# Placing two later triangular inverses behind a scan's first step, and giving each step's output matmuls a PSUM bank of their own

## The chip, the cores and the metric

The kernel runs on one core of one Trainium2 chip. The metric is the device time of one execution in microseconds (us), the median over several runs. The core has five engines with a queue each: TensorE (PE, with its weight loads shown apart as PEld), VectorE (DVE), ScalarE (ACT), GpSimd (POOL) and SyncE (SP, which issues the DMAs). An engine executes its queue in order, so an instruction that waits holds back all that stand behind it.

## What is computed

The reference is one layer of a diffusion trunk over 128 context tokens and 512 latent tokens of width 1024. Around two sub-layers stand RMS norms with shift, scale and gate. The first sub-layer sends one input projection to two mixers: an attention of 8 query heads, and RWKV-7 time mixing of 8 heads of width 64 in two directions. The second is a gated feed-forward block with a convolution of width 3 over the tokens. The part that matters here is the time mixing, which the reference writes token by token:

```python
sa = einsum('bhvk,bhk->bhv', s, -kk_t)
s = s * w_t + sa[..., None] * (kk_t * a_t) + v_t[..., None] * k_t
y = einsum('bhvk,bhk->bhv', s, r_t)
```

The layer returns both token streams, the context's keys and values, and the final states of the context's scans.

## The kernel before, in words

**Chunks instead of tokens.** The scan is taken in chunks of 64 tokens. Within a chunk the recursion is solved with the inverse of a 64 by 64 triangular matrix. Heads come in pairs, an even and an odd one on the two halves of the 128 partitions ("par"). There are three groups: `g0` (head pairs 0 and 1, 8 latent chunks), `ctx` (all four pairs, 2 context chunks) and `g1` (pairs 2 and 3, 8 latent chunks), walked in this order by each of the two directions. That makes 20 chunk steps for each direction.

**The inverses.** `inverse` (L829) makes the chunk inverses of one group. DVE transposes the group's matrix `LT` into `Lt` in four instructions (L845). `Ls` is formed from it (L854), and a row-by-row elimination follows (L870, L871), on DVE for `g0` and `ctx` and on POOL for `g1`. DVE transposes the result twice (`XT`, `XN`, L875 and L877). Eight copies put the diagonal blocks into `MT` (L889), each on DVE or ACT as the planner chose. Matmuls make `W` (L897), ACT copies it out (`Ws`, L901), matmuls make `B` (L909), and four copies bring `B` into `MT` (L912 to L915). The helper `cpy` makes such copies, so in the profile they stand on its line L377.

**Grams, decays, steps.** `s_gram` multiplies, for two chunks at once, the loaded rows `AK` (L964); it takes both banks of the PSUM ring `mi`, one for each par. DVE masks each into `GM` (L968) and ACT adds a block (L972). `s_decay` transposes the decayed rows into `DT` through one `mi` bank (L998). `s_chain` (L1033) is the dependent part of a step: it multiplies `GM` with the state and values `V_` (L1067), ACT copies that out as `Rt`, `MT` is applied (L1075), ACT scales the result to `U_` (L1080), `DT` is applied (L1089). Then the same generator issues the output: eight matmuls (L1099, L1103) into a fourth slot of the same PSUM bank `cp`. After them DVE adds the state update (L1113) into the next chunk's `V_`. The stream `out` (L1117) copies the output to `y` (first half of the steps) or adds it there (L1127), and then frees the slot (ring `yp`).

**What runs beside it.** `s_gemm2` computes the last input projections (L556, L570); their results are copied out (tile `e`, L377), stored (L464) and read back (L1265) for the attention. The attention's norms (L1289), scores (L1412), transposes (L1439) and weighted sums (L1460) follow, beside the scan, then the output projection (L1687), and from about 640 us on the feed-forward block (L1844, L2050).

**What sets the order.** Each piece of work is a generator that yields a request for an engine with an estimated duration, for a free slot of a ring, or for an event. A planner (`Flow`) resumes the generator whose request can start first, by estimated times and priorities. This gives the order of emission. A list scheduler then orders each engine's queue, by emission with boosts: `s_chain` has priority 0 and boost 200, `inverse` of `ctx` 0.1 and of `g1` 0.15 with boost 100, `s_gram` and `s_decay` 0.2, `out` 0.3 with boost 100. `behind` orders two instructions of one engine without a semaphore.

Of the kernel before, what the change touches and what calls it, by code (L numbers as in the profile page):

```python
# [47 lines left out]
def trunk(ctx: ExitStack, tc: tile.TileContext, a, o, dbg=None):  # L48
# [598 lines left out]

    G0, G1, CX = Group("g0", (0, 1), 2, 8), Group("g1", (2, 3), 2, 8), Group("ctx", (0, 1, 2, 3), 0, 2)
    groups = [G0, CX, G1]
    pt = [rc.tile([P, 4, 10], F32, name=nm("pt")) for _ in range(2)]  # L650
    bon = rc.tile([P, 10, 4], F32, name="bon")
    qm = [rf.tile([P, 10, 65], F32, name=nm("qm")) for _ in range(2)]
# [176 lines left out]
    def inverse(g, en, pl, mp, sfx, rg, bank):  # L829
        eng = ve if en == "V" else ge  # L830

        def W(n, k=1):
            return V(n, k=k) if en == "V" else G(0.99 * (k * 0.1 + 2.2e-3 * n))

        nu, LT = g.nu, g.LT
        for p in g.pairs:
            for d in range(2):
                yield ev_("ab", p, d)
        yield ring("inv" + sfx)
        Lt = pl.tile([P, 1024], F32, name=nm("Lt"), tag="i0" + sfx)  # L840
        for qd in range(4):
            pr = slice(32 * qd, 32 * qd + 32)
            t0 = 32 * (qd % 2)
            yield V(1024)
            ve.transpose(Lt[pr].rearrange("p (t s) -> p t s", s=32), LT[pr, :, t0:t0 + 32].rearrange("p u t -> p t u"))  # L845
        Ls = pl.tile([P, 32, 32], F32, name=nm("Ls"), tag="i1" + sfx)
        X = pl.tile([P, 1024], F32, name=nm("X"), tag="i2" + sfx)
        X3 = X.rearrange("p (t s) -> p t s", s=32)
        Lt3 = Lt.rearrange("p (t s) -> p t s", s=32)
        yield G(1.0)  # L850
        ge.memset(X, 0.0)
        ge.memset(X[:, ::33], 1.0)
        yield W(1024)
        eng.tensor_tensor(Ls, Lt3, Lt3.rearrange("p t s -> p s t"), ALU.add)  # L854

        yield A(496, k=12)
        Lf = Ls.rearrange("p t s -> p (t s)")
        se.copy(X[:, 32::66], Lf[:, 32::66])
        for i in range(2):
            for j in range(2):  # L860
                se.copy(X[:, 64 + 32 * i + j::132], Lf[:, 64 + 32 * i + j::132])
        for b in (4, 8, 16):
            for q in range(0, 32, 2 * b):
                se.copy(X3[:, q + b:q + 2 * b, q:q + b], Ls[:, q + b:q + 2 * b, q:q + b])
        tmp = pl.tile([P, 256], F32, name=nm("tmp"), tag="i3" + sfx)
        for s in range(1, 31):
            n = 31 - s
            yield W(2 * n * s, k=2)
            t3 = tmp[:, :n * s].rearrange("p (t j) -> p t j", j=s)
            eng.tensor_tensor(t3, Ls[:, s + 1:32, s:s + 1].to_broadcast([P, n, s]), X3[:, s:s + 1, 0:s].to_broadcast([P, n, s]), ALU.mult)  # L870
            eng.tensor_tensor(X3[:, s + 1:32, 0:s], X3[:, s + 1:32, 0:s], t3, ALU.add)  # L871
        XT = pl.tile([P, 1024], F32, name=nm("XT"), tag="i0" + sfx)
        XN = pl.tile([P, 1024], F32, name=nm("XN"), tag="i1" + sfx)
        yield V(1024)
        ve.transpose(XT, X)  # L875
        yield V(1024)
        ve.transpose(XN.rearrange("p (j u) -> p j u", u=32), X3.rearrange("p i j -> p j i"))  # L877
        XT3 = XT.rearrange("p (i u) -> p u i", u=32)
        XN3 = XN.rearrange("p (j u) -> p u j", u=32)
        MT = mp[0].tile([P, 2 * nu, 64], F32, name=nm("MT"), tag=mp[1] or "MT" + g.nm)  # L880
        g.MT = MT
        yield G(2.0)
        ge.memset(MT, 0.0)
        fw, bw = slice(0, nu), slice(nu, 2 * nu)
        qs_ = [(slice(64 * e, 64 * e + 32), slice(64 * e + 32, 64 * e + 64)) for e in range(2)]
        for e in range(2):
            q0, q1 = qs_[e]
            for dst, src in ((MT[q0, fw, 0:32], XT3[q0, fw]), (MT[q1, fw, 32:64], XT3[q1, fw]), (MT[q0, bw, 0:32], XN3[q0, bw]), (MT[q1, bw, 32:64], XN3[q1, bw])):
                e2 = yield VA(32 * nu)  # L889
                cpy(e2, dst, src)  # L890
        yield ring(rg)
        W3 = bank("W")[:, :32 * nu].rearrange("p (u j) -> p u j", j=32)
        for u in range(nu):
            if u % 4 == 0:
                yield T(0.5)
            for q0, q1 in qs_:
                te.matmul(W3[q1, u], lhsT=LT[q0, u, 32:64], rhs=XN3[q0, u], start=True, stop=True)  # L897
                te.matmul(W3[q0, u], lhsT=LT[q1, nu + u, 0:32], rhs=XT3[q1, nu + u], start=True, stop=True)
        yield A(32 * nu)
        Ws = pl.tile([P, 16, 32], F32, name=nm("Ws"), tag="i2" + sfx)  # L900
        se.copy(Ws[:, :nu], W3)  # L901
        flow.give(rg)
        yield ring(rg)
        B3 = bank("B")[:, :32 * nu].rearrange("p (u j) -> p u j", j=32)
        for u in range(nu):
            if u % 4 == 0:
                yield T(0.5)
            for q0, q1 in qs_:
                te.matmul(B3[q0, u], lhsT=Ws[q1, u], rhs=XT3[q1, u], start=True, stop=True)  # L909
                te.matmul(B3[q1, u], lhsT=Ws[q0, u], rhs=XN3[q0, nu + u], start=True, stop=True)  # L910
        for q0, q1 in qs_:
            e2 = yield VA(32 * nu)  # L912
            cpy(e2, MT[q0, fw, 32:64], B3[q0])
            e2 = yield VA(32 * nu, par=True)
            cpy(e2, MT[q1, bw, 0:32], B3[q1])  # L915
        flow.give(rg)
        flow.give("inv" + sfx)
        flow.done("inv", g.nm)
# [29 lines left out]
    def s_gram(d):  # L948

        mm = cm[:, C_MK + 128 * d:C_MK + 128 * d + 128]  # L950
        for g, i0, j, cc in two(d):
            keys = [(d, g.nm, i0, ci) for ci in cc]
            yield ev_("ak", *keys[1])
            yield ring(f"GM{d}")
            GM = rp2.tile([P, 2, 2, 2, 128], F32, name=nm("GM"), tag=f"GM{d}", bufs=2)
            yield ring("mi", 2)
            ps = [mi("gr").rearrange("p (s i t) -> p s i t", s=2, i=2) for _ in range(2)]
            yield T(1.75)
            for s, key in enumerate(keys):
                ak = akt[key]  # L960
                for i in range(2):
                    for par in range(2):
                        pr = HALF[par]
                        te.matmul(ps[par][:, s, i], lhsT=ak[pr, i, 1], rhs=ak[pr, i, 0], start=True, stop=True)  # L964
            for par in range(2):
                pr = HALF[par]
                yield V(512)
                ve.tensor_tensor(GM[:, :, par], ps[par], mm[:, None, None].to_broadcast([P, 2, 2, 128]), ALU.mult)  # L968
                flow.give("mi")
                yield A(256, k=2)  # L970
                for s, key in enumerate(keys):
                    se.copy(GM[pr, s, par, :, LO], akt[key][pr, :, 0, LO])  # L972
            for s, key in enumerate(keys):
                grams[key] = GM[:, s]
                flow.done("gm", *key)
# [53 lines left out]
            flow.done("set", g.nm)  # L1029

    cps, cpf = [], []

    def s_chain(d):  # L1033
        cp = cps[d]
# [7 lines left out]
        for g, i0, j, ci in walk(d):  # L1042
# [45 lines left out]
                    for par in range(2):  # L1088
                        order(par, te.matmul(cp[HALF[par], 2, i], lhsT=DT[:, i, HALF[par]], rhs=U_[par][:, i], start=True, stop=True))  # L1089
            flow.give(f"DT{d}")  # L1090
            yield ring(f"yp{d}")

            ak = akt.pop(key)
            yield T(0.6)

            for i in range(2):
                for par in range(2):
                    pr = HALF[par]
                    order(par, te.matmul(cp[pr, 3, i], lhsT=ak[pr, i, 0, HI], rhs=V_[par][pr, i], start=(i == 0), stop=False, skip_group_check=True))  # L1099
            for i in range(2):  # L1100
                for par in range(2):
                    pr = HALF[par]
                    order(par, te.matmul(cp[pr, 3, i], lhsT=GM[:, par, i, HI], rhs=U_[par][:, i], start=False, stop=True, skip_group_check=True))  # L1103
            flow.done("mm", *key)
            flow.add(0.3, out(g, d, i0, j, ci), 100)
            if not last and (g.nch - 1 - (j + 1)) <= j:
                yield ev_("mm", 1 - d, g.nm, i0, nxt)
            if upd:
# [5 lines left out]
            if last and g.outs[d] is not None and i0 == g.np - 2:  # L1114
                sy.dma_start(o["so"][d], g.outs[d])

    def out(g, d, i0, j, ci):  # L1117
        first = j < g.nch - 1 - j
        if not first:
            yield ev_("out", 1 - d, g.nm, i0, ci)  # L1120
        yv, yp = g.y[:, ci, i0:i0 + 2], cps[d][:, 3]
        if first:
            eng = yield OPT_E(128)
            cpy(eng, yv, yp)
        else:
            yield V(128)
            ve.tensor_tensor(yv, yv, yp, ALU.add)  # L1127
        flow.give(f"yp{d}")
        if j % 2:
            flow.give(f"GM{d}")  # L1130
            flow.give(f"AK{d}")
# [399 lines left out]
    rp2 = rp2p.__enter__()  # L1531
    flow.done("rp2")
    flow.add(PR_MOD1, s_mods1())
    for name, n in (("yp0", 1), ("yp1", 1), ("md", 1), ("GM0", 2), ("GM1", 2), ("DT0", 2), ("BD0", 1), ("BD1", 1), ("DT1", 2), ("AK0", 2), ("AK1", 2), ("gT", 2), ("set", 1), ("setx", 1)):
        flow.ring(name, n)
    rwkv = []
    for d in range(2):
# [678 lines left out]
```

## Time and profile before

| | us |
|---|---|
| median of 3 runs (lowest to highest) | 1103.17 (1098.99 to 1106.76) |
| profiled execution, its own time | 1104.36 |
| its span, first to last instruction | 1102.6 |
| mean granted TensorE clock | 0.94 of full speed |
| PE / DVE / ACT / POOL busy | 1019.5 / 790.7 / 563.4 / 507.4 |

A row of a timeline gives the start, the duration, the engine, the line, the operation, output and input, shapes and count, and in brackets the idle time before it with what ended that. A row of stages gives, for a stretch, the busy time of each engine with its number of instructions, then the granted TensorE clock, the DMA share and GB/s. A row of waits gives who waited, for whom, the us in total, how often, and the longest.

### The profile page before, as it was taken

The numbers are of one execution on the slowest core, as the hardware profiler recorded it, in microseconds if no ns is written. First come the engines' busy times: TensorE is split into PE (matmuls) and PEld (weight loads), VectorE is DVE, ScalarE is ACT, GpSimd is POOL, SyncE is SP. The second block draws the span as 40 slices with busy tenths as digits, with TensorE's granted clock in tenths as the row PEclk, the third lists the DMA queues.
The fourth block names the chain that finished last, engine by engine and source line by source line (L and its number), as shares of the span: only waits on it lengthen the run. The fifth ranks groups of instructions, "written<-read, shape, count | busy, mean of one in ns | idle before, by whom it ended". The sixth has DMA issues, their size and how long they took to land. (4 is left out here: it accounts for less than half of the span.)

```text
span 1102.6 us, 20567 instructions
## 1 busy us (share of the span) xinstructions
PE 1019.5 (92%) x8034; PEld 853.6 (77%) x8034; DVE 790.7 (72%) x1367; ACT 563.4 (51%) x1261; POOL 507.4 (46%) x446
## 2 busy tenths in 40 slices
PE   6999998778779999999999988999999998899997
PEld 3788776677665556777777888999999997788885
DVE  3536689989729777465774789999999999643324
ACT  4275433254654767476654764555555556334431
POOL 1234423567415204210202058788888888642330
PEclk8899998889857899799999999999999999899999
DMA  9414534640245684211061421222222223531202
GB/s 364 185 67 116 152 103 133 184 126 21 97 150 194 212 267 136 68 59 61 9 229 74 153 90 44 88 89 94 77 77 78 78 99 112 193 113 58 95 1 96
DMA packets 70433, 127.84 MB, mean 116 GB/s; under 512 B 15664, under 2 KB 41776, under 8 KB 67264
## 3 DMA queue, kind: packets, MB, share of 16 engines
q1 hardware_dynamic: 70336, 126.53, 34.4%
q8 instruction: 63, 1.03, 0.4%
q14 instruction: 34, 0.28, 0.1%
HBM read 105.00 MB, written 21.51 MB: 115 GB/s over the span
## 5 line engine op out<-in xcount | busy, mean ns | idle before, releaser
L1807 POOL TENSOR_TENSOR w<-raw,w 128x512 fp32r<-128x512 f32 (+1 forms) x84 | 153.9, 1839 | 142.6 <-ACT w L1806 121.4
L2050 PE MATMUL dn<-w,ah 128*128 128x512 f32 x660 | 155.7, 398 | 7.9 <-DVE c L1850 7.9
L2050 PEld LDWEIGHTS dn<-w,ah 128*128 128x128 f32 x660 | 125.1, 190 | 38.3 <-issue 8.3
L1844 PE MATMUL up<-tq,w 128*128 128x324 f32 x960 | 150.2, 312 | 2.8 <-DVE x L1989 2.8
L1844 PEld LDWEIGHTS up<-tq,w 128*128 128x128 f32 x960 | 145.2, 190 | 3.1 <-DVE x L1989 3.1
L1844 PE MATMUL up<-hq,w 128*128 128x324 f32 x864 | 137.0, 313 | 4.8 <-ACT w L1806 2.3
L1844 PEld LDWEIGHTS up<-hq,w 128*128 128x128 f32 x864 | 129.6, 188 | 7.8 <-DVE up L1992 4.6
L1807 POOL TENSOR_TENSOR w<-sw,w 128x512 fp32r<-128x512 f32 x80 | 122.4, 1551 | 8.6 <-ACT w L1806 8.6
L1924 DVE TENSOR_TENSOR ah<-act,ah 128x644 fp32r<-128x644 f32 x42 | 58.7, 1415 | 75.8 <-ACT ah L1923 75.8
L1848 ACT ACTIVATE c<-up,pv 128x322 f32<-128x322 f32 x86 | 52.1, 620 | 97.3 <-DVE up L1992 55.6
L432 POOL TENSOR_TENSOR lo<-raw,hi 128x1024 fp32r<-128x1024 f32 x17 | 42.7, 2509 | 68.4 <-ACT hi L430 66.9
L1063 POOL TENSOR_TENSOR SP<-vse,pt 64x128 f32<-64x128 f32 x36 | 14.3, 398 | 128.4 <-DVE vse L1113 127.7
L1923 ACT CAST ah<-act 128x644 fp32r<-128x644 f32 x44 | 31.8, 732 | 76.4 <-PE dn L2050 76.3
L1806 ACT CAST w<-raw 128x512 fp32r<-128x512 f32 (+1 forms) x86 | 63.2, 748 | 5.0 <-PE dn L2050 2.8
L964 PE MATMUL gr<-AK 64*128 64x128 f32 x320 | 47.4, 329 | 11.8 <-ACT DT L377 4.5
L964 PEld LDWEIGHTS gr<-AK 64*128 64x128 f32 x320 | 38.8, 222 | 21.4 <-ACT DT L377 4.7
L1687 PE MATMUL op<-wo,m 128*128 128x512 f32 x192 | 48.3, 404 | 1.7 <-DVE m L1681 1.0
L1849 DVE SCALAR_TENSOR_TENSOR c<-up,pv,c 128x322 f32<-128x322 f32 x86 | 46.5, 543 | 3.8 <-ACT c L1848 3.8
L1806 ACT CAST w<-sw 128x512 fp32r<-128x512 f32 x80 | 47.5, 620 | 2.7 <-PE up L1844 2.7
L1850 DVE SCALAR_TENSOR_TENSOR c<-up,pv,c 128x322 f32<-128x322 f32 x86 | 46.6, 545 | 0.8
L1687 PEld LDWEIGHTS op<-wo,m 128*128 128x128 f32 x192 | 36.7, 194 | 10.5 <-DVE m L1681 1.4
L968 DVE TENSOR_TENSOR GM<-gr,cm 128x512 f32<-128x512 f32 x40 | 26.8, 684 | 21.7 <-PE gr L964 21.3
(335 smaller groups left out, 2485.1 us busy)
## 6 DMA issues: line engine op xcount, KB each, us to landing
wm<-in_wmod SPq DMA_DIRECT2D x24, 1024.0 KB, 6.6
raw<-in_up SPq DMA_DIRECT2D x44, 512.0 KB, 3.3
raw<-in_down SPq DMA_DIRECT2D x22, 512.0 KB, 3.3
AK<-arkd SPq DMA_DIRECT2D x40, 256.0 KB, 4.4
raw<-in_wfm SPq DMA_DIRECT2D x10, 512.0 KB, 5.9
arkd<-AR SPq DMA_DIRECT2D x8, 640.0 KB, 3.7
xT<-in_xT SPq DMA_DIRECT2D x8, 320.0 KB, 6.1
arkd<-BK SPq DMA_DIRECT2D x16, 160.0 KB, 3.5
```

What stands on the lines that cost most here:

```text
L432: ge.tensor_tensor(lo, raw, hi.bitcast(F32), ALU.subtract)
L964: te.matmul(ps[par][:, s, i], lhsT=ak[pr, i, 1], rhs=ak[pr, i, 0], start=True, stop=True)
L1687: te.matmul(acc[hf], lhsT=m2[xi][:, k - k0], rhs=wo[k // 2][wi][k % 2][:, 512 * hf:512 * hf + 512], start=(n_mm == 0 and pi == 0), stop=(n ...
L1806: se.copy(hi, raw)
L1807: eng.tensor_tensor(lo, raw, hi.bitcast(F32), ALU.subtract)
L1844: te.matmul(ps, lhsT=wq[wi][:, 128 * k:128 * k + 128], rhs=xq[xi][:, k], start=(first and k == 0 and pi == 0), stop=(last and k == 3 and p ...
L1848: se.activation(c, src[..., 1:H2N - 1], AF.Identity, scale=pv[:, col + 1:col + 2], bias=pv[:, col + 3:col + 4])
L1849: ve.scalar_tensor_tensor(c, src[..., 0:H2N - 2], pv[:, col:col + 1], c, ALU.mult, ALU.add)
L1850: ve.scalar_tensor_tensor(c, src[..., 2:H2N], pv[:, col + 2:col + 3], c, ALU.mult, ALU.add)
L1923: se.copy(t[:, 0, 1:645], act[:, k, 1:645])
L1924: eng.tensor_tensor(t[:, 1, 1:645], act[:, k, 1:645], t[:, 0, 1:645].bitcast(F32), ALU.subtract)
L2050: return [te.matmul(ps, lhsT=(ah, al)[xi][:, p0:p0 + 128], rhs=w2[wi][:, k % 2], start=(k == 0 and pi == 0), stop=(k == 21 and pi == 2)) f ...
```

## The change

It has two parts. The first: the inverses of `ctx` and `g1` wait in the planner until the inverse of `g0` is done and the first masks of `g0` exist in both directions. Their transposes are also ordered behind these masks and behind DVE's share of the copies of `B`, which are collected in `starts`. Those copies are now fixed, two on ACT and two on DVE. The second: the eight output matmuls of a step leave `s_chain` for the stream `out`, which now takes a bank of the ring `mi` for them and gives it back after the copy or the addition. The ring `yp` is gone; the counter `om` keeps the outputs of one direction in order, and the event `mm` is set when the output matmuls are issued.

```diff
-            ve.transpose(Lt[pr]..., LT[pr, :, t0:t0 + 32]...)
+        if g is not G0:
+            yield ev_("inv", "g0")
+            for d in range(2):
+                yield ev_("gm", d, "g0", 0, (1, G0.nch - 2)[d])
...
+            tr = ve.transpose(Lt[pr]..., LT[pr, :, t0:t0 + 32]...)
+            if g is not G0:
+                for m in starts:
+                    behind(tr, m)
...
-            e2 = yield VA(32 * nu)
-            cpy(e2, MT[q0, fw, 32:64], B3[q0])
-            e2 = yield VA(32 * nu, par=True)
-            cpy(e2, MT[q1, bw, 0:32], B3[q1])
+            yield A(32 * nu)
+            se.copy(MT[q0, fw, 32:64], B3[q0])
+            yield V(32 * nu, par=True)
+            m = ve.tensor_copy(MT[q1, bw, 0:32], B3[q1])
+            if g is G0:
+                starts.append(m)
...
-                ve.tensor_tensor(GM[:, :, par], ps[par], mm..., ALU.mult)
+                m = ve.tensor_tensor(GM[:, :, par], ps[par], mm..., ALU.mult)
+                if g is G0 and j == 0:
+                    starts.append(m)
...
     def s_chain(d):
...
-            yield ring(f"yp{d}")
-            ak = akt.pop(key)
-            yield T(0.6)
-            (eight matmuls into cp[:, 3], from ak and V_, then GM and U_)
-            flow.done("mm", *key)
-            flow.add(0.3, out(g, d, i0, j, ci), 100)
+            flow.add(0.15, out(g, d, i0, j, ci, akt.pop(key), GM, V_, U_), 100)
...
-    def out(g, d, i0, j, ci):
+    def out(g, d, i0, j, ci, ak, GM, V_, U_):
+        n = nout[d]
+        nout[d] += 1
+        yield ev_("om", d, n)
+        yield ring("mi")
+        yield T(0.6)
+        yp = mi("yp")[:, :128].rearrange("p (i v) -> p i v", i=2)
+        (the same eight matmuls into yp, each behind the one before of its par)
+        flow.done("om", d, n + 1)
+        flow.done("mm", d, g.nm, i0, ci)
         first = j < g.nch - 1 - j
         if not first:
             yield ev_("out", 1 - d, g.nm, i0, ci)
-        yv, yp = g.y[:, ci, i0:i0 + 2], cps[d][:, 3]
+        yv = g.y[:, ci, i0:i0 + 2]
...
-        flow.give(f"yp{d}")
+        flow.give("mi")
```

## Rows read from the trace of the kernel before

**Rows 1.** Two stages: up to the attention's start, and the dense one behind it.

```profile
205.00:330.00 125.00, 96.79 (x1403) 86.01 (x1402) 92.75 (x131) 61.56 (x157) 64.17 (x95) 0.81 0.39 113
...
330.00:580.00 250.00, 238.67 (x2514) 170.58 (x2514) 177.33 (x461) 150.98 (x460) 61.80 (x118) 0.91 0.41 138
```

**Rows 2.** Stretches of 5 us around the first group's start; the clock is behind POOL.

```profile
225.00:230.00 5.00, 2.50 (x19) 2.30 (x18) 4.28 (x3) 4.94 (x8) 2.01 (x2) 1.00 1.21 215
230.00:235.00 5.00, 4.61 (x139) 4.31 (x140) 2.76 (x1) 4.34 (x18) 5.00 (x4) 0.53 0.24 43
235.00:240.00 5.00, 5.00 (x36) 5.00 (x36) 4.97 (x4) 0.00 (x0) 4.36 (x12) 0.79 0.35 108
...
245.00:250.00 5.00, 4.33 (x25) 4.14 (x26) 4.35 (x6) 2.68 (x16) 4.61 (x6) 0.73 0.15 52
```

**Rows 3.** Waits of PE from 205 to 330 us.

```profile
PE B L909 <- ACT Ws L901: 2.9, 1, 2.9
...
PE gr L964 <- DVE GM L968: 3.5, 2, 3.3
...
PE dt L998 <- DVE GM L968: 2.8, 2, 1.7
PE cp L1067 <- ACT y L377: 2.1, 2, 1.5
```

**Rows 4.** Timeline of DVE: transposes, the copies of B, and masks.

```profile
221.51 7.79 DVE L845 STREAM_TRANSPOSE Lt<-LT 32x1024 f32<-32x1024 f32 x4
232.24 3.24 DVE L561 TENSOR_SCALAR sg<-sg 128x640 f32<-128x640 f32 x1 [2.94 <-ACT sg L558]
235.40 8.08 DVE L845 STREAM_TRANSPOSE Lt<-LT 32x1024 f32<-32x1024 f32 x4
243.51 1.39 DVE L377 COPY MT<-B 32x512 f32<-32x512 f32 x2
244.93 0.69 DVE L968 TENSOR_TENSOR GM<-gr,cm 128x512 f32<-128x512 f32 x1
...
273.90 0.68 DVE L968 TENSOR_TENSOR GM<-gr,cm 128x512 f32<-128x512 f32 x1
```

**Rows 5.** Timeline of ACT: the first group's copies.

```profile
219.65 4.42 ACT L377 COPY MT<-XT 32x512 f32<-32x512 f32 x4 [9.25 <-DVE XT L875]
...
224.53 4.45 ACT L377 COPY MT<-XN 32x512 f32<-32x512 f32 x4
...
229.78 0.56 ACT L901 COPY Ws<-W 128x512 f32<-128x512 f32 x1
...
233.85 0.57 ACT L377 COPY MT<-B 32x512 f32<-32x512 f32 x1
244.93 0.58 ACT L377 COPY MT<-B 32x512 f32<-32x512 f32 x1 [10.51 <-DVE MT L377]
```

**Rows 6.** Timeline: end of a step's outputs on PE, update, output copy, next step.

```profile
262.67 0.22 PE L1089 MATMUL cp<-uvo,DT 128*64 128x64 f32 x1
...
263.43 0.22 PE L1103 MATMUL cp<-uvo,GM 128*64 128x64 f32 x1
...
267.50 0.29 DVE L1113 TENSOR_TENSOR vso<-cp,SP 64x128 f32<-64x128 f32 x1
...
267.88 0.27 ACT L377 COPY y<-cp 128x128 f32<-128x128 f32 x1 [2.05 <-DVE vso L1113]
...
268.20 0.27 PE L1067 MATMUL cp<-vse,GM 128*64 128x64 f32 x1 [0.63 <-ACT y L377]
```

**Rows 7.** What DVE's state update (L1113) waited for, over the whole span.

```profile
  PE cp L1103: 10.9, 10
```

**Rows 8.** Timeline of POOL: the third inverse starts.

```profile
229.39 2.87 POOL L854 TENSOR_TENSOR Ls<-Lt 128x1024 f32<-128x1024 f32 x1 [2.99 <-DVE Lt L845]
```

**Rows 9.** Timeline of ACT: the third inverse's copies ahead of the last projection's.

```profile
303.60 4.23 ACT L377 COPY MT<-XN 32x512 f32<-32x512 f32 x4
...
309.00 0.37 ACT L377 COPY e<-tm 128x256 f32<-128x256 f32 x1
```

More of the change, by code (lines that the diff above doesn't have):

```diff
@@ L649, in trunk @@
     groups = [G0, CX, G1]
+    starts = []
     pt = [rc.tile([P, 4, 10], F32, name=nm("pt")) for _ in range(2)]
@@ L844, in inverse @@
             yield V(1024)
-            ve.transpose(Lt[pr].rearrange("p (t s) -> p t s", s=32), LT[pr, :, t0:t0 + 32].rearrange("p u t -> p t u"))
+            tr = ve.transpose(Lt[pr].rearrange("p (t s) -> p t s", s=32), LT[pr, :, t0:t0 + 32].rearrange("p u t -> p t u"))
+            if g is not G0:
+                for m in starts:
+                    behind(tr, m)
         Ls = pl.tile([P, 32, 32], F32, name=nm("Ls"), tag="i1" + sfx)
@@ L967, in s_gram @@
                 yield V(512)
-                ve.tensor_tensor(GM[:, :, par], ps[par], mm[:, None, None].to_broadcast([P, 2, 2, 128]), ALU.mult)
+                m = ve.tensor_tensor(GM[:, :, par], ps[par], mm[:, None, None].to_broadcast([P, 2, 2, 128]), ALU.mult)
+                if g is G0 and j == 0:
+                    starts.append(m)
                 flow.give("mi")
@@ L1031, in trunk @@
     cps, cpf = [], []
+    nout = [0, 0]
+    for d in range(2):
+        flow.done("om", d, 0)
     def s_chain(d):
@@ L1090, in s_chain @@
             flow.give(f"DT{d}")
-            yield ring(f"yp{d}")
-            ak = akt.pop(key)
-            yield T(0.6)
[L1096 to L1103, printed above, removed]
-            flow.done("mm", *key)
-            flow.add(0.3, out(g, d, i0, j, ci), 100)
+            flow.add(0.15, out(g, d, i0, j, ci, akt.pop(key), GM, V_, U_), 100)
             if not last and (g.nch - 1 - (j + 1)) <= j:
@@ L1115, in s_chain @@
                 sy.dma_start(o["so"][d], g.outs[d])
-    def out(g, d, i0, j, ci):
+    def out(g, d, i0, j, ci, ak, GM, V_, U_):
[5 more added lines that the diff above has]
+        yp = mi("yp")[:, :128].rearrange("p (i v) -> p i v", i=2)
+        prev = [None, None]
+        for st in range(2):
+            for i in range(2):
+                for par in range(2):
+                    pr = HALF[par]
+                    if st == 0:
+                        mm = te.matmul(yp[pr, i], lhsT=ak[pr, i, 0, HI], rhs=V_[par][pr, i], start=(i == 0), stop=False, skip_group_check=True)
+                    else:
+                        mm = te.matmul(yp[pr, i], lhsT=GM[:, par, i, HI], rhs=U_[par][:, i], start=False, stop=True, skip_group_check=True)
+                    if prev[par] is not None:
+                        behind(mm, prev[par])
+                    prev[par] = mm
+        flow.done("om", d, n + 1)
+        flow.done("mm", d, g.nm, i0, ci)
         first = j < g.nch - 1 - j
@@ L1533, in trunk @@
     flow.add(PR_MOD1, s_mods1())
-    for name, n in (("yp0", 1), ("yp1", 1), ("md", 1), ("GM0", 2), ("GM1", 2), ("DT0", 2), ("BD0", 1), ("BD1", 1), ("DT1", 2), ("AK0", 2), ("AK1", 2), ("gT", 2), ("set", 1), ("setx", 1)):
+    for name, n in (("md", 1), ("GM0", 2), ("GM1", 2), ("DT0", 2), ("BD0", 1), ("BD1", 1), ("DT1", 2), ("AK0", 2), ("AK1", 2), ("gT", 2), ("set", 1), ("setx", 1)):
         flow.ring(name, n)
```

## The prediction

> **What bounds the kernel now.** I read the stages first. From 205 to 330 us PE is busy for 96.79 of 125 us, so 28.2 us lie idle, at a mean granted clock of 0.81; from 330 to 580 us it is busy for 238.67 of 250 [rows 1]. The reader is to see two regimes: up to 330 us PE waits for chains of small work on other engines, behind it PE is nearly full and everything ends when its work is through. So an idle microsecond removed before 330 us brings the end forward by about as much, if nothing takes its place; shortening a chain that lies inside the full stretch brings little.
>
> Next the waits of PE in the first regime. Four belong to the code that changes: `B` waits 2.9 us for `Ws`, the grams 3.5 and the decay transposes 2.8 for masks, the next step's first matmul 2.1 for an output copy [rows 3]. They sum to 11.3 us; what else makes up the 28.2 is not touched directly.
>
> Then the timelines, for what is late. DVE transposes the two later groups in two sets, 7.79 us from 221.51 and 8.08 us from 235.40, and only at 243.51 does it reach its two copies of `B`, at 244.93 the first mask, at 273.90 the last of the four first masks of `g0` [rows 4]. ACT had made its first copy of `B` at 233.85 already, and idled 10.51 us for the next [rows 5]. So the second set of transposes stands ahead of the first group's start. The first set stands beside ACT's eight copies of `XT` and `XN` (219.65 to 228.98) and the `Ws` behind them at 229.78 [rows 5].
>
> Last the clock: the stretch 225 to 230 has PE busy for half of it, and the next two run at 0.53 and 0.79 of full speed; behind the 3.3 us wait for the mask that ended at 245.6 the stretch from 245 runs at 0.73 [rows 2 to 4]. An idle gap is paid twice here.
>
> **The change, part by part.** Sixteen us of transposes move behind four masks; none is added or removed. Directly, the copies of `B` can follow `sg` at 235.5 and no longer at 243.5: 8.1 us, the second set [rows 4]. Besides, DVE is free while ACT makes its eight copies of 1.1 us; the planner may put up to half on DVE (0.70 each there [rows 4]), which brings `Ws` forward by 0 to 4.4 us. What of this is PE's:
> - `B` waiting for `Ws`: 2.9 us. With `Ws` 4.4 us earlier the wait is gone. I take 2.9; the bound is 0, if all copies stay on ACT.
> - Grams and transposes waiting for masks: 3.5 + 2.8 us. The first goes with the second set. The 2.8 are masks of later steps; they go if the grams keep their lead, and stay if sixteen us of transposes now stand ahead of those masks. I take 6.3, the bound is 3.5.
> - The clock behind the two gaps: 4.61 us at 0.53, 5.00 at 0.79 and 4.33 at 0.73 [rows 2] are 2.2 + 1.05 + 1.2 = 4.4 us more than at full clock. I take all; the bound is 0, if other gaps keep the clock down.
>
> Where do the transposes' waiters go? The POOL inverse, which began at 229.39 [rows 8], begins some 20 us later, behind up to eight transposes, and ends that much later. Its consumers are the third group's first steps, behind 12 steps of each direction, and the loads for the second modulation, with slack on the far side of 330 us; I cost this at nothing. If that cover went, the price would be those 20 us in the walk. One thing moves favourably: at 303.60 ACT still copies this inverse's blocks and reaches the last projection's copy `e` only at 309.00 [rows 9], on which the attention's loads hang. A later inverse gets out of its way: 0 to 5 us, of which I count none, since the copies then stand before the attention's norms.
>
> The outputs. Their eight matmuls cost PE the same as before. In the old place they lie between the last `DT` matmul (262.89) and the update, which waited for their end (263.65); the update's waits on them sum to 10.9 us in 10 cases [rows 6, 7], so 0.8 us of each step's dependent chain goes. The output copy was read from the same bank: it waited 2.05 us for the update's second half, and the next step's first matmul waited 0.63 us for it [rows 6]. With a bank of their own these links are cut, but the next step still needs the update, which had ended at 267.79, 0.36 us before the copy. Of PE's 2.1 us I take 1.4. In the dense stretch other work fills such gaps, so I count nothing there.
>
> New: the outputs now share the two `mi` banks with grams, decays and gate products; a gram needs both. The trace has no such wait. Nearest rows: the matmuls (0.76 us) and the copy (0.27) hold a bank 1.0 us at best; in the old order 4.9 us passed from the last `DT` matmul's end (262.89) to the copy's start, and 5.3 to its end at 268.15 [rows 6]. Most of that stay was waiting for the update, which goes. There are 40 outputs, and 20 grams. A stay costs PE only if nothing else stands at its head; it may even cost nothing, since the grams run ahead with two `GM` buffers for each direction. I take 1 us in all; the ends are 0 and 20 grams x 5.3 = 106 us, the latter absurdly far since PE has other work.
>
> The four copies of `B` are now two on ACT and two on DVE. In the trace ACT's second copy started at 244.93, just behind DVE's pair, which ended at 244.90 [rows 4, 5], so by rows four alternate copies take 0.57 + 0.69 + 0.58 + 0.70 = 2.5 us. The Trainium skill, "PSUM — Partial Sum Buffer", section "PSUM bank collisions raise a hardware error", says that two engines may use one bank together if they are in different quadrants of 32 partitions; by that rule ACT's and DVE's copies, which lie in different quadrants, could run in pairs, in about 1.3 us, and the sum below would be 1.2 us better. The trace disagrees (the 10.51 us wait), though it does not show whether the bank or the tile `MT` made it.
>
> Sum: 2.9 + 6.3 + 4.4 + 1.4 - 1.0 = 14.0 us. The profiled execution took 1104.36 us, so 1090.4 for it. It stands 1.2 us above the median of the runs, so the forecast against that is 1089 to 1090; I say 1090, within 1079 to 1100 (the bounds without a gain for `Ws`, later masks and clock leave 3.9 us; with the 5 us of the copy `e` and earlier second-direction steps that fill more of the 28.2 idle us, some 24).
>
> **Rivals.** *The gap moves.* Before 330 us PE's filling is the projection, whose amount is fixed. If the two gaps close, it runs out earlier, and PE idles before the attention starts, because that hangs on the copy `e` behind ACT's queue (309.00, [rows 9]) and not on PE. For it: that copy already stands behind 4.23 us of `MT` copies. Against it: the scan's second direction, whose first masks end only at 274.6 [rows 4], can start some 30 us earlier and gives PE other work. Time: 1103, give or take 4.
>
> *The outputs starve the grams.* Place: ring `mi` in the full stretch, where each second-half output holds its bank while it also waits for the other direction's output and for DVE. The gram behind it waits for both banks, PE's queue stands, and the chain behind has no `GM`. Against it: the update no longer keeps the copy back. It decides from 14.0 / 20 = 0.7 us of PE standing per gram; at 1.25 us the kernel is 1% slower. With 2 us per gram, twice the shortest stay, the price is 40 us: 1104 - 14 + 40, about 1130. The Trainium skill's rule on the same page, to guard PSUM by bank and quadrant and not by address, speaks for this: an output that fills 128 of 512 columns shuts out a gram from the whole bank.
>
> *The second direction counts more.* Two chains from 240 us instead of one until 275 fill most of the 28 idle us before the dense stretch, and the clock stays up: 25 to 35 us, about 1075.
>
> That the change does not do what it says I give no weight: the order behind the masks is within one engine's queue, and the new bank is another tile.
>
> **How the numbers follow.** A measurement of this kernel tells some 1% (11 us) from no change. Forecast 0.52, the gap moves 0.24, starved grams 0.16, the larger gain 0.08. A gain of 11 us lies at 1092.1; I put four fifths of the forecast below that, so faster is 0.8 x 0.52 + 0.08 = 0.49, the same 0.11 + 0.24 = 0.35, slower 0.16. The range goes from 1075 (half of the larger gain) to 1113 (all but the starved grams), leaving out 0.16 + 0.03. The forecast's own range is 1079 to 1100.
>
> **What would show it.** Right: the copies of `B` and the first four masks end before 245 us, with all eight transposes behind them; PE's waits for `Ws` and for the first masks are gone, the clock from 230 to 250 us is near full; the update waits for L1089 and not for an output matmul; PE's idle time before the attention's scores falls by some 10 us, and the feed-forward starts 10 to 15 us earlier with its own length unchanged. Wrong: idle time of the same size now stands before the attention's start; or grams wait for output copies in the full stretch; or a later start of the third inverse holds up the scan's third group.

## The result and the profile after

The changed kernel took 1129.11 us (median of 4 runs, 1128.02 to 1131.38) against 1102.70 for the kernel before (four runs beside it): ratio 1.0241, 95% interval 1.0204 to 1.0278. It is slower by 26 us; I had forecast 1090. The profiled execution's span is 1126.2 us, 23.6 above that of before. Lines of the inverse, grams, chain and outputs have other numbers now; the names of the tiles are the same.

The two stages of [rows 1] after the change (length, then busy time of PE, PEld, DVE, ACT and POOL, clock, DMA share, GB/s):

```profile
205.00:330.00 125.00, 101.18 (x1206) 89.51 (x1207) 86.16 (x138) 56.30 (x170) 58.37 (x81) 0.80 0.35 100
330.00:580.00 250.00, 223.00 (x2601) 162.87 (x2598) 168.28 (x422) 148.44 (x421) 72.11 (x132) 0.85 0.39 127
```

PE has 4.4 us more in the first stage and 15.7 less in the second, which was nearly full before. First what went as predicted. DVE's timeline, start and duration, as [rows 4]:

```profile
235.38 0.68 DVE L924 COPY MT<-B 32x512 f32<-32x512 f32 x1
236.10 0.69 DVE L979 TENSOR_TENSOR GM<-gr,cm 128x512 f32<-128x512 f32 x1
236.82 0.70 DVE L924 COPY MT<-B 32x512 f32<-32x512 f32 x1
241.47 0.69 DVE L979 TENSOR_TENSOR GM<-gr,cm 128x512 f32<-128x512 f32 x1 [2.66 <-PE gr L975]
...
265.54 1.29 DVE L979 TENSOR_TENSOR GM<-gr,cm 128x512 f32<-128x512 f32 x2 [3.81 <-PE gr L975]
266.75 15.87 DVE L851 STREAM_TRANSPOSE Lt<-LT 32x1024 f32<-32x1024 f32 x8
```

The copies of `B` are done at 237.5 in place of 244.9, the first direction's two masks at 236.8 and 242.2. The second direction's come only at 265.54, a few us ahead of their old place, and behind them stand all eight transposes. From 242.2 to 265.5 DVE does only two later masks and four halves of state updates. The 5 us stretches that answer to [rows 2] (PE busy, granted clock, DMA share, GB/s):

```profile
225.00:230.00 5.00, 3.33 (x45) 1.00 1.17 269
230.00:235.00 5.00, 3.91 (x136) 0.63 0.54 94
235.00:240.00 5.00, 5.00 (x29) 0.68 0.38 129
240.00:245.00 5.00, 5.00 (x41) 1.00 0.09 32
245.00:250.00 5.00, 5.00 (x45) 1.00 0.08 27
```

The gap behind 240 us is closed and the clock there is full. From 230 to 240 us it is not: 0.63 and 0.68. Summed as in the prediction (busy time, times what the clock lacks of 1), the stretches of its clock term lose some 3 us where they lost 4.4, so little more than 1 us of that term came. PE's waits from 205 to 330 us, against [rows 3], and what the state update waited for, against [rows 7]:

```profile
PE cp L1083 <- DVE vso L1115: 6.0, 4, 2.7
...
PE yp L1133 <- DVE GM L979: 3.4, 3, 1.7
PE B L918 <- ACT Ws L910: 2.8, 1, 2.8
...
PE dt L1011 <- DVE GM L979: 1.1, 1, 1.1
...
PE gr L975 <- DVE GM L979: 1.0, 1, 1.0
```

```profile
  PE cp L1105: 9.6, 7
  ACT y L377: 1.2, 1
  PE yp L1133: 1.0, 1
```

Grams and decay transposes wait 2.1 us for masks in place of 6.3, but the output matmuls, which now need a bank of the same ring, wait 3.4 us for masks themselves (`yp`). `B` still waits 2.8 for `Ws`. The update waits for the `DT` product now and hardly for the outputs (1.0 us); the next step's first product waits for the update (6.0 us) and not, as in [rows 6], for the output copy (2.1). So part of the waiting has changed its place and not gone. Now the loss. GpSimd's start, which answers to [rows 8], and its last elimination:

```profile
282.76 2.81 POOL L863 TENSOR_TENSOR Ls<-Lt 128x1024 f32<-128x1024 f32 x1 [18.99 <-DVE Lt L851]
...
361.55 0.25 POOL L880 TENSOR_TENSOR X<-X,tmp 128x30 f32<-128x30 f32 x1
```

It begins 53.4 us late. The second modulation's weights come through two buffers that hold the two later inverses' inputs (`LTctx`, `LTg1`), and the stream that forms its products (`s_mods1`) waits for both inverses. Their first two loads, on SP's queue, which were at 294.3 and 319.6 before:

```profile
347.04 0.33 SPq L583 DMA_DIRECT2D wm<-in_wmod  x1
372.62 0.57 SPq L583 DMA_DIRECT2D wm<-in_wmod  x1
```

The products, before and then after: line, count, ns of one, first and last start:

```profile
L603 PE MATMUL gemv<-wm,sc x128: 589/617/1062, 334.5 to 416.4; 128*32 128x512 f32 x128
```

```profile
L603 PE MATMUL gemv<-wm,sc x128: 592/617/1063, 383.7 to 469.0; 128*32 128x512 f32 x128
```

They start 49 us late. PE by stage (busy, clock, DMA share, GB/s), before and then after:

```profile
205.00:300.00 95.00, 72.67 (x986) 0.88 0.36 100
300.00:450.00 150.00, 136.12 (x1622) 0.83 0.58 191
450.00:620.00 170.00, 164.99 (x1476) 0.93 0.24 85
```

```profile
205.00:300.00 95.00, 78.74 (x1003) 0.87 0.40 111
300.00:450.00 150.00, 121.94 (x1404) 0.66 0.43 139
450.00:620.00 170.00, 157.80 (x1584) 0.99 0.31 110
```

Busy time times the mean clock of the stretch is an estimate of what PE got done, in us at full clock (called work from here on): 63.9, 113.0 and 153.4 before, 68.5, 80.5 and 156.2 after. So 4.6 are gained ahead of 300 us, 32.5 lost from 300 to 450, 2.8 regained: 25.2 us of work less by 620 us, and the span is 23.6 longer. Of the 32.5 us, 14.18 busy us less at a clock of 0.83 make 11.8; the other 20.7 are the 121.94 busy us that ran at 0.66 and not at 0.83. So PE lost more by its clock in this stretch than by standing idle.

### The profile page after: what moved, and what is told of

Its sections match the earlier page's. It is cut to its first block, busy times and chain, and to the rows that moved or that the text cites. A ratio compares the mean times of both kernels' runs of the same rounds, so it can differ in the third digit from the quotient of the medians.

```text
span 1126.2 us, 20598 instructions
## 1 busy us (share of the span) xinstructions
PE 1029.5 (91%) x8034; PEld 866.0 (77%) x8034; DVE 784.0 (70%) x1366; ACT 565.1 (50%) x1261; POOL 512.6 (46%) x447
## 5 line engine op out<-in xcount | busy, mean ns | idle before, releaser
L1867 PEld LDWEIGHTS up<-hq,w 128*128 128x128 f32 x864 | 132.1, 191 | 5.7 <-DVE up L2015 3.0
L1079 POOL TENSOR_TENSOR SP<-vse,pt 64x128 f32<-64x128 f32 x36 | 17.3, 482 | 117.1 <-DVE vse L1115 114.8
L975 PEld LDWEIGHTS gr<-AK 64*128 64x128 f32 x320 | 41.2, 224 | 10.0 <-DVE GM L979 2.2
```

Source lines behind the costliest of these rows:

```text
L1867: te.matmul(ps, lhsT=wq[wi][:, 128 * k:128 * k + 128], rhs=xq[xi][:, k], start=(first and k == 0 and pi == 0), stop=(last and k == 3 and p ...
```

## The experiments

Theory W: the loss is the wait for the second direction's masks, which makes both later inverses late. Rival O: it is the outputs in the grams' ring. (The context inverse eliminates on VectorE, DVE; the other later one, `g1`, on GpSimd, POOL.)

**e1, the waits alone** (the kernel before, with the new waits and copies; outputs as before). 

> The kernel before with the waits alone: the later inverses' transposes stand behind the first inverse's copies and both directions' first masks, a step's outputs stay in their old bank. Theory W (the loss is the wait: VectorE idles in front of the second direction's masks, both later inverses start 38 to 53 us later, and their elimination then runs beside attention's norms): 1120 to 1135 us, the GpSimd inverse's Ls after 270 us, TensorE at half clock for most of 305 to 385 us. Rival O (outputs in the grams' ring hold up the grams and so the loss comes from the outputs): 1085 to 1103 us.

Measured: 1117.64 us, ratio 1.0147 (1.0087 to 1.0208). That lies between the two ranges, 2.4 us below W's and far above O's: the waits alone cost about three fifths of the loss.

**e2, the outputs alone** (the kernel after without the waits and with the copies of `B` free again).
```
-        if g is not G0:
-            yield ev_("inv", "g0")
-            for d in range(2):
-                yield ev_("gm", d, "g0", 0, (1, G0.nch - 2)[d])
...
-                for m in starts:
-                    behind(tr, m)
```


> The kernel after with the waits undone: outputs stay in the grams' ring and have a stream of their own, the transposes go back ahead of the first inverse's copies. Theory W: 1093 to 1105 us, Ls on GpSimd near 230 us as before, a clock above .8 in 360 to 400 us. Rival O: 1122 to 1132 us, with gram or gram-mask waits of over 10 us in all on TensorE between 270 and 500 us.

Measured: 1103.46, ratio 1.0021 (0.9987 to 1.0056). Alone, the new bank is worth nothing either way. With the waits it costs: e1 is 11 us faster than the full change. In e1 the second direction's masks are done at 260.3 and not at 266.8, and its POOL follows the transposes 6.4 us sooner than in the kernel after:

```profile
276.32 4.55 POOL L863 TENSOR_TENSOR Ls<-Lt 128x1024 f32<-128x1024 f32 x1 [12.14 <-DVE Lt L851]
```

So O has a place of some 11 us, in company with W's wait. By the trace the masks that the transposes wait for come some 6 us later with the outputs in the grams' ring. Besides, from 285 to 415 us output matmuls stand at the head of PE's queue in the kernel after for 10.5 us (5.8 for a state update, 3.4 for masks, 1.3 for `U_`); none does in e1. How the 11 us divide is not shown.

**e3, one direction's masks; e4, the copies alone.**
```
-            for d in range(2):
-                yield ev_("gm", d, "g0", 0, (1, G0.nch - 2)[d])
+            yield ev_("gm", 0, "g0", 0, 1)      # e3; e4: neither
...
-                if g is G0 and j == 0:
+                if g is G0 and j == 0 and d == 0:   # e3; e4: no masks in starts
```


> The kernel after with one wait less: the transposes stand behind the first inverse's copies and the first direction's two masks, no longer behind the second direction's. Theory W: the eight transposes start near 242 us in place of 267, the GpSimd inverse's Ls near 250 to 258 us, and two thirds or more of the loss goes: 1085 to 1108 us. Rival O: 1122 to 1132 us. A third theory L (any start of the later inverses after their old one costs its full length, so 20 us of delay cost 20 us): 1108 to 1118 us.

> The kernel after with the waits for all masks taken away: the transposes stand behind the first inverse's copies alone, in front of the first direction's second mask. Theory W: transposes from some 238 us, Ls on GpSimd near 246 to 252 us, 1085 to 1105 us. Rival O: 1122 to 1132 us. Theory L (each us of delay costs one): 1106 to 1115 us.

Measured: e3 1090.99, ratio 0.9889 (0.9855 to 0.9923); e4 1097.78, ratio 0.9941 (0.9909 to 0.9972). Both are faster than the kernels before and after. W holds: e3 differs from the kernel after by the wait for the second direction's masks alone. O falls as the main cause; L falls, since in e3 POOL starts 30 us later than before and the time is 12 us shorter. Its DVE, POOL, modulation products, and PE by stage:

```profile
243.22 15.93 DVE L850 STREAM_TRANSPOSE Lt<-LT 32x1024 f32<-32x1024 f32 x8
```

```profile
259.24 2.77 POOL L862 TENSOR_TENSOR Ls<-Lt 128x1024 f32<-128x1024 f32 x1 [20.05 <-DVE Lt L850]
```

```profile
L603 PE MATMUL gemv<-wm,sc x128: 589/593/1061, 341.7 to 413.2; 128*32 128x512 f32 x128
```

```profile
205.00:300.00 95.00, 78.08 (x967) 0.86 0.35 97
300.00:450.00 150.00, 133.90 (x1797) 0.87 0.58 196
450.00:620.00 170.00, 162.45 (x1420) 0.98 0.26 93
```

The products start 7 us late, not 49, and the stretch from 300 to 450 us lost nothing (116.5 us of work against 113.0).

**e5, the context inverse alone waits** (`if g is CX` in place of `if g is not G0` in e3). 

> The kernel after, with the context inverse's transposes alone behind the first inverse's copies and the first direction's two masks; the GpSimd inverse's four transposes wait for nothing, as before. Theory W (the loss is the later inverses' start, the gain the closed gaps in front of 275 us): the GpSimd inverse starts again near 230 us, the context one near 250 us, and the gain stays: 1075 to 1092 us. Rival: the early transposes hold up the first inverse's copies again and the gain is lost with the loss: 1098 to 1106 us.

Measured: 1092.33, ratio 0.9898 (0.9842 to 0.9954), GpSimd's start at 229.59. The gain stays, 0.3 us above the upper end of its range; it is no better than e3's, though GpSimd starts 30 us sooner.

Why late inverses cost was next, with two theories: D, VectorE's elimination in the way of attention's norms; G, GpSimd's late end and the products behind it.

**e6 and e7, one of the two late** (in e3, that inverse waits for both directions). 

> The kernel of one direction's masks, with the context inverse (VectorE) alone waiting for the second direction's masks too. Theory D (what costs is VectorE: the context inverse's elimination running beside attention's norms): 1108 to 1128 us. Theory G (what costs is the GpSimd inverse ending late, with what waits for its buffers, the modulation products of 334 to 417 us before): 1086 to 1098 us.

> The kernel of one direction's masks, with the GpSimd inverse alone waiting for the second direction's masks too. Theory D: 1086 to 1098 us. Theory G: 1108 to 1128 us, modulation products after 380 us.

Measured: e6 1114.18, ratio 1.0104 (1.0030 to 1.0179), its products from 361.7 us; e7 1120.22, ratio 1.0144 (1.0077 to 1.0212), where its products start is not known. Each theory missed one of the two. Either lateness costs, 23 and 29 us against e3, so neither theory alone holds; both fit a stream that waits for the later of two.

**e8, no elimination on VectorE** (the kernel after; the context inverse's 60 operations are left out).
```
-        for s in range(1, 31):
+        for s in (() if g is CX else range(1, 31)):
```


> The kernel after, with both waits, but the context inverse's 60 elimination operations on VectorE (about 50 us of its time) left out, so the context inverse's numbers are not computed. Theory D: the loss goes with them, 1075 to 1100 us, though the GpSimd inverse still ends near 360 us. Theory G: 1115 to 1130 us.

Measured: 1128.28, ratio 1.0229 (1.0169 to 1.0290). D falls as the whole price: the 60 operations are 29.2 us of busy VectorE in the kernel after, spread over some 50, and without them the time is the same. The test is not quite clean. Attention's last transpose of q comes 9 us sooner (381.2 against 390.1), but the products come 11 us later, and the two may cancel. Its products:

```profile
L603 PE MATMUL gemv<-wm,sc x128: 589/617/1061, 394.9 to 471.2; 128*32 128x512 f32 x128
```

**e10, neither elimination** (both later inverses' left out: `range(1, 31) if g is G0 else ()`). 

> The kernel after, with both waits, but both later inverses' eliminations left out (60 operations each on VectorE and GpSimd, so these two inverses are not computed). The transposes still end near 283 us, the inverses by 310 us. Theory G: the modulation products start by 330 us again and the loss goes: 1075 to 1100 us. Rival (the late transposes or the second direction's late masks cost by themselves): 1115 to 1130 us, as with VectorE's elimination alone left out (1128.28).

Measured: 1084.50, ratio 0.9830 (0.9799 to 0.9860). The waits and the late transposes (271 us) are all there, and the loss is gone once the inverses end early. GpSimd also has 60 operations less; no run takes away these alone, so their lateness and their own time are not told apart. Products and stages:

```profile
L603 PE MATMUL gemv<-wm,sc x128: 589/617/1062, 333.8 to 407.1; 128*32 128x512 f32 x128
```

```profile
205.00:300.00 95.00, 80.19 (x1046) 0.86 0.35 95
300.00:450.00 150.00, 133.81 (x1682) 0.84 0.59 197
450.00:620.00 170.00, 164.44 (x1494) 0.99 0.26 93
```

**e9, the products late, the inverses as before.**
```
+        yield ev_("qk", 4)
...
+                    behind(mm, lastq[-1])    # each product behind the last transpose of q
```


> The kernel before, its inverses where they were, with the modulation products (the 128 gemv products of the stretch from 334 us) ordered behind the last transpose of attention's q, some 40 us later. Theory G (what the late inverses cost is that these products, which fill TensorE beside attention's norms, come when TensorE is full): 64 products, 12.97 us of TensorE, leave 334 to 375 us and come later: 1110 to 1122 us. Rival: they fit in later for nothing, 1098 to 1106 us, and the price of the late inverses lies elsewhere.

Measured: 1116.25, ratio 1.0115 (1.0080 to 1.0150):

```profile
L603 PE MATMUL gemv<-wm,sc x128: 589/592/632, 386.1 to 468.2; 128*32 128x512 f32 x128
```

```profile
205.00:300.00 95.00, 76.59 (x1005) 0.88 0.34 90
300.00:450.00 150.00, 130.91 (x1579) 0.76 0.49 163
450.00:620.00 170.00, 155.42 (x1467) 0.99 0.29 101
```

This is theory G's range. Held back to where the change puts them, the products alone cost 13 us, with no inverse late.

**e11, old bank; e12, GpSimd's transposes first** (e11: e5 without the new bank; e12: in e3 the context inverse also waits for `g1`'s transposes). 

> The kernel before with the context inverse's transposes alone behind the first inverse's copies and the first direction's two masks, outputs in their old bank. If the outputs' bank is worth nothing (as the kernel with it alone, ratio 1.002), as fast as the kernel with both: 1085 to 1098 us. If the closed gaps pay only with the outputs out of the chain's way: 1098 to 1106 us.

> The kernel of one direction's masks, with the GpSimd inverse's four transposes in front of the context inverse's four: GpSimd starts some 8 us sooner, near 251 us, VectorE's elimination at the same time. Theory G: the modulation products start up to 8 us sooner, 1080 to 1092 us. Rival (the later of the two ends decides and it is VectorE's): no change, 1088 to 1094 us.

Measured: e11 1094.58, ratio 0.9909 (0.9878 to 0.9940): the gain is the order's, not the bank's. e12 1094.94, ratio 0.9921 (0.9891 to 0.9951): GpSimd starts at 250.99, its products at 345.0 against e3's 341.7, no gain; the rival's side, a little above its range.

**e13 and e14, half of the products** (64 of the 128 are left out by `if hh == 0`, in the kernel after and before). 

> The kernel after with every second half of the 16 half-blocks of modulation products left out (64 of the 128 products; their inputs are still loaded), so these sums are not complete. Theory G (after 400 us TensorE is full, so a product costs its own length there: .142 us each at full clock, 9 us for 64): 1116 to 1122 us. Rival (the loss lies in the starved stretch itself, and what comes behind it is not the bound): 1126 to 1131 us.

> The kernel before with the same 64 products left out. Theory G: they lie mostly beside attention's norms, where TensorE has room, so 0 to 5 us: 1098 to 1104 us. Rival (a product costs the same wherever it lies): as much as in the kernel after.

Measured: e13 1113.21, ratio 1.0074 (1.0041 to 1.0108), below both ranges: 15.9 us less than the kernel after took, 18 by the two ratios. e14 1086.26, ratio 0.9822 (0.9779 to 0.9865), 19.2 less than the kernel before beside it. Theory G was wrong here: the same products cost no less in their old place, so they were not free filling there. Why 64 products are worth 16 to 19 us, when all 128 in their old place show 24 us of busy PE, is not settled.

**e15, products behind the context inverse alone** (`yield ev_("inv", "ctx")`, one buffer). 

> The kernel after, with the modulation products waiting for the context inverse alone and loaded through its one buffer, not for the GpSimd inverse too. Theory G: their first starts some 30 us sooner, near 355 us in place of 384, though one buffer spreads the rest: 1112 to 1124 us. Rival: 1126 to 1131 us.

Measured: 1150.77, ratio 1.0417 (1.0363 to 1.0470). A miss of both. The first product starts at 367, but one buffer draws them out to 504 us. Nor is the rest as it was: `W` and `B` of the GpSimd inverse use the same bank (`md`) as the products, and its last copy of `B` starts at 411.7 and no longer at 382.9. So e15 does not test what it was made for.

```profile
L603 PE MATMUL gemv<-wm,sc x128: 589/617/1062, 367.4 to 503.9; 128*32 128x512 f32 x128
```

What is common to them all is PE's work (the same three stretches, against before) beside the span of the same execution. The third column is the start of attention's last wide score product. e13 and e14 do less work than the others, and of e7 there is no trace to compare.

| kernel | products start, us | last wide scores, us | work by 620 us | span |
|---|---|---|---|---|
| before | 334.5 | 563.8 | 0 | 0 |
| e15 | 367.4 | 611.4 | -36.1 | +44.1 |
| e8 | 394.9 | 590.2 | -23.0 | +24.4 |
| after | 383.7 | 589.4 | -25.2 | +23.6 |
| e9 | 386.1 | 583.7 | -9.6 | +15.7 |
| e1 | 383.6 | 582.4 | -17.1 | +15.0 |
| e6 | 361.7 | 568.8 | -7.0 | +2.8 |
| e2 | 322.2 | 555.7 | -2.2 | -1.0 |
| e4 | 344.7 | 559.4 | +9.6 | -6.4 |
| e5 | 331.9 | 549.5 | +3.4 | -9.7 |
| e12 | 345.0 | 557.2 | +7.7 | -9.7 |
| e11 | 331.1 | 558.4 | +6.0 | -10.3 |
| e10 | 333.8 | 548.4 | +13.8 | -17.7 |
| e3 | 341.7 | 551.7 | +12.5 | -18.2 |

Work that is not done by 620 us is added at the end, one for one within 8 us. This says where the time is lost, not why. The products' start alone does not order the kernels: in e2 they start 12 us sooner than before, for no gain. The end of attention's scores does better; it moves with the span within 8 us. By 620 us all products and scores are done in both kernels; what the kernel after lacks is the output projection behind the attention, 60 matmuls against 133.

## Why the prediction was wrong

*The step that failed* is the sentence that the GpSimd inverse's consumers are "the third group's first steps ... and the loads for the second modulation, with slack on the far side of 330 us; I cost this at nothing". Three things in it were off.

- The delay. I wrote some 20 us; it is 53 for GpSimd, since the wait holds for the second direction's masks as well, and those come at 265.5. I had read their old end (274.6) and assumed that they would come some 30 us sooner; they came 6 to 8 us sooner.
- The cover. The second modulation has no slack: in the kernel before its products start at 334.5 us, as soon as the inverses are through, and are part of what keeps PE busy. Late inverses leave PE without them (300 to 450 us: 121.94 us busy at 0.66, against 136.12 at 0.83). So the second of my two regimes was full only as long as its work was released in time. e10 takes away the lateness and the loss goes; e9 delays the products alone and costs 13 us.
- The fallback price, "those 20 us in the walk". The walk does not end late: its last first-product starts at 540 us, against 547 before. What is late is attention: its wide scores start 24.5 us later and then take as long as before (176 and 175 us). Before, then after:

```profile
L1412 PE MATMUL s<-K,qs x128: 302/309/636, 388.6 to 563.8; 128*128 128x320 f32 x128
L1435 PE MATMUL s<-K,qs x128: 302/309/636, 413.1 to 589.4; 128*128 128x320 f32 x128
```

The list of consumers also lacked one. The context group's values go into a pool (`rp3`) that opens where the GpSimd inverse's pool closes, and their load moved with that inverse's end. Before, then after:

```profile
330.53 0.63 SPq L1016 DMA_DIRECT2D vse<-vvd  x1
378.77 0.58 SPq L1029 DMA_DIRECT2D vse<-vvd  x1
```

In the kernel after, the walk stands from its sixteenth step (362.5 us) to its seventeenth (387.2) and loses the lead that the change had given it; before, the seventeenth started at 395.4. It is not what parts this kernel from e3, where the seventeenth starts at 387.4.

The price of the wait for the second direction is 1129.11 less e3's 1090.99, 38 us. The products' place is worth 13 of it, if what e9 cost from the kernel before holds here too. The other 25 go when the eliminations go (e10), and not with VectorE's alone (e8). They show as attention's delay, but what of the work behind the late inverses delays it, no run separates; this cause stays open.

*The gain*, forecast at 14.0 us, is there in the versions that start the inverses earlier: 12 us in e3, 12 in e5. By terms: the waits of grams and transposes for masks shrank (6.3 to 2.1 us, with 3.4 new ones at the outputs); of the clock's 4.4 us little more than 1 came; the 2.9 us of `B` stayed, because all eight copies of `XT` and `XN` stayed on ACT, which was the bound I named and did not take. That 12 is near 14 is in part luck: of e3's 12.5 us of work only 3.2 lie ahead of 300 us (4.6 in the kernel after), the rest comes later, in stretches that the sum did not price.

*The outputs* were forecast at 1.4 less 1.0 us; alone they measure nothing (e2), and PE's waits at grams come to 3.1 us from 285 to 415. So the rival of starved grams is wrong as it was put, in the full stretch, and that its number, 1130, came out is luck. With the waits the outputs cost some 11 us (the kernel after less e1).

*The gap moves* saw that the projection would run out earlier and PE idle behind it; that came true (the last copy `e` of [rows 9] starts at 291.9 and not at 309.0), but the gap is 32 us of work and not of the gain's own size, and copy `e` is not what holds it open: it came 17 us sooner, the wide scores 24.5 us later. *The second direction counts more* fell with its masks at 265.5.

## What to carry to other kernels

Before work is put behind a wait, list everything that waits for its end, buffers freed there included, and look up in the trace when each of those starts: a consumer that starts as soon as it can may have no slack, however far off it is. Look too at what else opens when the work is through, such as a pool in the place of its tiles. When several things are waited for, price the last of them, by where it will come in the new order. And compare PE's busy time times its clock by stage; the stage that lost it says where to look sooner than the waits do.

## What the runs showed of the hardware

The four copies of `B` follow one another as they did before: ACT's second started at 236.10, behind DVE's first (235.38 to 236.06):

```profile
233.17 0.57 ACT L922 COPY MT<-B 32x512 f32<-32x512 f32 x1 [0.27 <-PE B L919]
236.10 0.58 ACT L922 COPY MT<-B 32x512 f32<-32x512 f32 x1 [2.36 <-DVE MT L924]
```

In both kernels no copy of `B` on one of the two engines overlaps one on the other, in any of the three inverses.

The Trainium skill, "PSUM — Partial Sum Buffer", section "PSUM bank collisions raise a hardware error", says that two engines may use one bank at the same time if they are in different quadrants. The trace shows copies that take turns, as the sum had it, and no run tells whether the bank or the tile `MT` orders them.
